# Scores of two heads at once, their low key halves as pairs of 64-row matmuls

## The chip, the cores and the metric

The kernel runs on one core of one Trainium2 chip. The metric is the device time of one execution in microseconds: from three executions the median was 1884.23 us (1883.11 to 1885.26). A separate execution was taken with the hardware profiler on; all rows below are from it.

The engines by their names in the profile: PE is the matmul engine (PEld its weight loads), DVE the vector engine, ACT the scalar engine, POOL the general one, SP issues transfers.

## The reference, cut to what matters

Two layers work on 256 tokens and 256 context tokens of width 2048: a Fourier layer and then an attention layer. The change lies in the second. Its attention has 64 query heads of width 64 in 8 groups that share one key head each. A query sees the tokens within 128 positions and all of the context, and a learned sink value joins each softmax.

```python
def _attend_with_sink(q, k, v, sink, mask=None):
    s = jnp.einsum('bqhgd,bkhd->bhgqk', q, k).astype(jnp.float32) * (ATTN_HEAD_DIM ** -0.5)
    if mask is not None:
        s = jnp.where(mask, s, NEG_INF)
    sk = jnp.broadcast_to(sink.astype(jnp.float32)[None, :, :, None, None], s.shape[:-1] + (1,))
    p = jax.nn.softmax(jnp.concatenate([s, sk], axis=-1), axis=-1)[..., :-1]
    return jnp.einsum('bhgqk,bkhd->bqhgd', p.astype(v.dtype), v)
```

The branch is multiplied by `silu(z)`, multiplied by the output weights, and added to the residual.

## The kernel before

Everything is float32. A matmul takes the reduced type `F32R`, and precision is kept by splitting an operand into a high part (`S.copy` into `F32R`, on ACT, line 60) and a low part (`V.tensor_tensor` subtract, on DVE, line 61). A product is then three matmuls (`mm3`, lines 73 to 75): high by high, high by low, low by high. Low by low is left out.

**Attention operands.** For each key head `hk`, `prep_kk` copies the 64 rows of the keys' high part into both halves of a 128-row tile `kkh`, and the low part into both halves of `kkl` (512 keys: 256 tokens, 256 context). `q_turn` makes the queries of two heads: `qa` holds the even head's high part in rows 0 to 63 and its low part in rows 64 to 127, `qb` holds the odd head's high part in rows 64 to 127 and its low part in rows 0 to 63. One 128-row matmul of `qa` by `kkh` so gives high by high plus low by high, and one of `qa` by `kkl` gives high by low plus low by low.

**Stages of one head** `i` (there are 64):

- `stage_s` (line 797): for each of two blocks of 128 queries a bank of PSUM takes the two matmuls (lines 810 and 811). DVE adds the mask and reduces the maximum (line 812, with a small row that reads the result). ACT takes the exponentials (Exp, line 815, twice, and `es`, line 816, once), DVE adds and inverts (817, 818), and ACT scales the two blocks (Copy, line 820). Result: the probabilities `p`.
- `stage_t` (line 823): eight transposes on PE (line 830) into two banks, then each is split into `ph` (ACT) and `pl` (DVE).
- `stage_o` (line 837): eight matmuls of the values by `ph` and `pl` (lines 844, 845) into one bank, copied out by ACT (`ot`, line 850) and added by DVE (851).

**Fillers.** Between the stages `filler()` calls `emit_unit`, which emits the next unit of other matmuls: an eighth of the query projection of the following key head (12 matmuls of 512 columns), half of a block of z (24 matmuls of 256 columns), or, at the end, a part of the output projection. Each unit needs a weight half split by `half_split` (`wh` on ACT, `wl` on DVE, 128 x 1024). A finished projection is copied by ACT (line 688) and rotated on POOL; a finished z block takes one `th` on ACT.

**Order.** The loop over `i` (line 870) emits: `stage_s(i)`, `stage_o(i - 2)`, a filler, `stage_t(i - 1)`, a filler. The tile framework schedules this program order against its own timeline when the kernel is built: an instruction may move forward past others that are not ready there. What results is one fixed order for each engine. PSUM has eight banks, all in one pool (`psum()`); the probabilities `p`, `ph` and `pl` have two buffers each for each name.

Of the kernel before, what the change touches and what calls it, by code (L numbers as in the profile page):

```python
# [16 lines left out]
P = 128  # L17
# [11 lines left out]
def tile_dit(ctx: ExitStack, tc: tile.TileContext, a: dict, out: bass.AP):  # L29
    nc = tc.nc  # L30
    V, S, PE, GP = nc.vector, nc.scalar, nc.tensor, nc.gpsimd
# [8 lines left out]
    def psum():  # L40
        return pp.tile([P, 512], F32, tag="ps", name="ps")
# [17 lines left out]
    def split(h, l, src):  # L59
        S.copy(h, src)  # L60
        V.tensor_tensor(l, src, h.bitcast(F32), op=ALU.subtract)  # L61
# [85 lines left out]
    with tc.tile_pool(name="st", reuse_waits="tile", bufs=1, side="right") as st:  # L147
# [55 lines left out]
        for nb in range(4):  # L203
# [11 lines left out]
            for j in range(4):  # L215
                o = psum()
# [93 lines left out]
    for g in range(G):  # L310
# [38 lines left out]
        if g == 0:  # L349
            o = psum()  # L350
# [79 lines left out]
    with tc.tile_pool(name="yp", reuse_waits="tile", bufs=32) as ypool:  # L430
# [19 lines left out]
        with tc.tile_pool(name="zp", reuse_waits="tile", bufs=2) as zp:  # L450
# [29 lines left out]
            for b in range(4, NB):  # L480
# [3 lines left out]
                o = psum()  # L484
# [32 lines left out]
        for i in range(32):  # L517
            sw, kg = i // 16, i % 16
            if kg == 0:
                o = [psum() for _ in range(8)]  # L520
# [29 lines left out]
    o = psum()  # L550
# [8 lines left out]
    o = psum()  # L559
# [27 lines left out]
    with tc.tile_pool(name="h1", reuse_waits="tile", bufs=16) as h1p:  # L587
# [3 lines left out]
        with tc.tile_pool(name="kvp", reuse_waits="tile", bufs=2) as kvp:  # L591
# [12 lines left out]
            o = [[psum() for _ in range(2)] for _ in range(4)]  # L604
# [25 lines left out]
            for hp in range(4):  # L630
                o = psum()
# [10 lines left out]
        with tc.tile_pool(name="at", reuse_waits="tile", bufs=2) as at:  # L642

            kk, qq, obs, szs = {}, {}, {}, {}
# [144 lines left out]
            def emit_y(blk):  # L789
                if blk not in szs or (blk, 1) not in obs or blk in ydone:  # L790
                    return
                ydone.add(blk)
                if blk % 2 == 0:
                    y1.append(act())
                V.scalar_tensor_tensor(y1[blk // 2][:, (blk % 2) * N : (blk % 2 + 1) * N], obs[blk, 1], 0.5, szs.pop(blk), op0=ALU.mult, op1=ALU.mult)

            def stage_s(i):
                hk, blk, hh = i // 8, i // 2, i % 2
                p2, pr = (blk % 4) // 2, blk % 2
                kkh, kkl = kk[hk]  # L800
                q2 = qq[hk, p2][hh]
                pt = at.tile([P, 2, 512], F32, tag="p", name="p")
                mx = at.tile([P, 2], F32, tag="mx", name="mx")
                sm = at.tile([P, 2], F32, tag="sm", name="sm")
                es = at.tile([P, 2], F32, tag="es", name="es")
                so = []
                for tb in range(2):
                    o = psum()
                    st = q2[:, (pr * 2 + tb) * P : (pr * 2 + tb + 1) * P]
                    PE.matmul(o, st, kkh, start=True, stop=False)  # L810
                    PE.matmul(o, st, kkl, start=False, stop=True)  # L811
                    V.tensor_tensor_reduce(o, o, mask[:, tb, :], -0.125, nsink[:, i : i + 1], ALU.add, ALU.min, mx[:, tb : tb + 1])  # L812
                    so.append(o)
                for tb in range(2):
                    S.activation(pt[:, tb, :], so[tb], AF.Exp, bias=mx[:, tb : tb + 1], scale=-1.0, accum_out=sm[:, tb : tb + 1])  # L815
                S.activation(es, mx, AF.Exp, bias=sink[:, i : i + 1])
                V.tensor_tensor(sm, sm, es, op=ALU.add)
                V.reciprocal(sm, sm)
                for tb in range(2):
                    S.activation(pt[:, tb, :], pt[:, tb, :], AF.Copy, scale=sm[:, tb : tb + 1])  # L820
                return pt

            def stage_t(pt):
                res = []
                for kp in range(2):
                    o = psum()
                    for kt in range(2):
                        for tb in range(2):
                            c = (kp * 2 + kt) * P
                            PE.transpose(o[:, (kt * 2 + tb) * P : (kt * 2 + tb + 1) * P], pt[:, tb, c : c + P], ident)  # L830
                    ph = at.tile([P, 512], F32R, tag="ph", name="ph")
                    pl = at.tile([P, 512], F32R, tag="pl", name="pl")
                    split(ph, pl, o)
                    res.append((ph, pl))
                return res

            def stage_o(i, pts):
                hk, blk, hh = i // 8, i // 2, i % 2
                oo = psum()
                for kb in range(4):  # L840
                    ph, pl = pts[kb // 2]
                    q = slice((kb % 2) * N, (kb % 2 + 1) * N)
                    st = v2[kb][hk // 4][:, (hk % 4) * P : (hk % 4 + 1) * P]
                    PE.matmul(oo[:, 0:N], st, ph[:, q], start=kb == 0, stop=False)  # L844
                    PE.matmul(oo[:, 0:N], st, pl[:, q], start=False, stop=kb == 3)  # L845
                if hh == 0:
                    obs[blk, 0] = at.tile([P, N], F32, tag="ob", name="ob", bufs=4)
                ob = obs[blk, 0]
                t = at.tile([64, N], F32, tag="ot", name="ot", bufs=1)
                S.copy(t, oo[64:128, 0:N])  # L850
                V.tensor_tensor(ob[hh * 64 : hh * 64 + 64, :], oo[0:64, 0:N], t, op=ALU.add)
                if hh == 1:
                    obs[blk, 1] = ob
                    emit_y(blk)
# [7 lines left out]
            def filler():  # L862
                j = slot[0]
                slot[0] += 1
                emit_unit()
                if defer and defer[0][0] + 2 < j:
                    defer.pop(0)[1]()

            pts, ptt = {}, {}
            for i in range(66):  # L870
                if i % 8 == 0:
                    while defer:
                        defer.pop(0)[1]()
                if i < 64:
                    pts[i] = stage_s(i)
                if i >= 2:
                    stage_o(i - 2, ptt.pop(i - 2))
                filler()
                if 1 <= i < 65:
                    ptt[i - 1] = stage_t(pts.pop(i - 1))  # L880
                filler()


        with tc.tile_pool(name="fin", reuse_waits="tile", bufs=1) as fp:
# [28 lines left out]
            o = [[psum() for _ in range(2)] for _ in range(2)]  # L913
# [12 lines left out]
            o = [psum() for _ in range(2)]  # L926
# [148 lines left out]
```

## Time and profile before

| | |
|---|---|
| median of three executions | 1884.23 us |
| the profiled execution | 1881.67 us |
| its span, first to last instruction | 1879.8 us |
| granted clock of PE, mean | 0.988 |
| the attention loop | about 1186 to 1715 us of the span |

A row of a group gives source line, engine, operation, output and input tile, shape and count, then busy time and the mean duration of one. A row of the timeline begins with its start in us and its duration. Matmuls are pipelined: one lasts longer than the distance to the start of the next, so it is that distance which tells what a matmul costs. Text in square brackets is idle time of the engine before the row and what ended it.

The costliest groups around the change, over the whole run:

```profile
L812 DVE CUSTOM_DVE_ANT_0 ps<-ps,mask,nsink 128x512 f32<-128x512 f32 x128 | 92.0, 753 | 10.9 <-PE ps L811 10.6
L815 ACT ACTIVATE p<-ps,mx 128x512 f32<-128x512 f32 x128 | 87.3, 687 | 21.3 <-DVE mx L812 20.3
L830 PE MATMUL ps<-ident,p 128*128 128x128 f32 x512 | 68.1, 273 | 0.2 <-ACT p L820 0.2
L844 PE MATMUL ps<-ph,act 128*128 128x256 f32 x256 | 66.9, 281 | 0.7 <-ACT ph L60 0.7
```

### The profile page before, as it was taken

To read this page: it belongs to the slowest core of one execution; us is meant where nothing else is said; L and a number is where in the kernel's file an instruction comes from. 1 tells how busy PE (TensorE), PEld (TensorE's weight loads), DVE (VectorE), ACT (ScalarE), POOL (GpSimd) and SP (SyncE) were. 2 spreads that over 40 slices of the span, in tenths; PEclk is the share of its full clock that TensorE was granted. 3 is DMA by queue.
4 is the path that set the end of the run, shared out by engine and by line. 5 is a ranking of instruction groups with operands and counts; after the bars stand their busy time and mean duration, and the time that the engine had idled before them with its cause. 6 is when DMAs were issued, how large, how long until landed. Compare 5 with 4: busy or idle time off the path is not lost.

```text
span 1879.8 us, 27439 instructions
## 1 busy us (share of the span) xinstructions
PE 1835.5 (98%) x10433; PEld 1583.7 (84%) x10433; DVE 1396.9 (74%) x2711; ACT 929.7 (49%) x1602; POOL 240.5 (13%) x206
## 2 busy tenths in 40 slices
PE   6899999999999999999999999999999999999997
PEld 4479999888888888888888787889989989998886
DVE  4469999787777789687984835788778787787455
ACT  3334444442222233324221524888888888887343
POOL 0034444200000000000000001112221220200001
PEclk8899999999999999999999999999999999999999
DMA  9965555656665546763575323333333333434543
GB/s 365 387 258 201 200 202 189 233 218 232 244 232 214 224 179 256 269 236 134 224 270 222 129 90 135 135 132 115 129 118 135 113 135 126 167 132 169 192 179 135
DMA packets 60533, 359.67 MB, mean 191 GB/s; under 512 B 7601, under 2 KB 7745, under 8 KB 25329
## 3 DMA queue, kind: packets, MB, share of 16 engines
q1 hardware_dynamic: 49104, 324.83, 46.7%
q0 software_dynamic: 6720, 25.34, 3.6%
q10 hardware_dynamic: 4576, 7.74, 1.3%
q8 instruction: 82, 1.34, 0.3%
q14 instruction: 51, 0.41, 0.1%
HBM read 345.30 MB, written 12.59 MB: 190 GB/s over the span
## 4 chain that ended last, share of the span: by engine, by line
PE 88%; DVE 4%; DMA 3%; issue 2%; ACT 1%; POOL 1%; ACTq 0%; POOLq 0%; DVEq 0%; SPq 0%
PE ps L73 25%; PE ps L74 25%; PE ps L75 25%; PE ps L830 3%; PE ps L845 2%; PE ps L844 2%; PE ps L811 1%; PE ps L810 1%; DMA raw<-in_awp 1%; DMA raw<-in_wu 1%; PE ps L180 1%; POOL wm L122 1%; DVE mt L239 1%; DVE wpl L61 1%; DVE wml L61 0%
## 5 line engine op out<-in xcount | busy, mean ns | idle before, releaser
L61 DVE TENSOR_TENSOR wl<-raw,wh 128x1024 fp32r<-128x1024 f32 x333 | 423.7, 1274 | 291.1 <-ACT wh L60 288.8
L60 ACT CAST wh<-raw 128x1024 fp32r<-128x1024 f32 x333 | 349.4, 1051 | 566.2 <-PE ps L74 507.0
L74 PE MATMUL ps<-act,wh 128*128 128x512 f32 x1024 | 398.3, 389 | 0.0
L73 PE MATMUL ps<-act,wh 128*128 128x512 f32 x1024 | 394.1, 389 | 0.0
L75 PE MATMUL ps<-act,wl 128*128 128x512 f32 x1024 | 391.1, 389 | 0.0
L73 PEld LDWEIGHTS ps<-act,wh 128*128 128x128 f32 x1024 | 192.2, 188 | 39.8
L75 PEld LDWEIGHTS ps<-act,wl 128*128 128x128 f32 x1024 | 192.2, 188 | 39.9
L74 PEld LDWEIGHTS ps<-act,wh 128*128 128x128 f32 x1024 | 192.2, 188 | 39.8
L417 DVE CUSTOM_DVE_ANT_0 raw<-raw,cb 128x512 f32<-128x512 f32 x256 | 172.5, 688 | 16.4 <-DMA raw<-in_adw 12.6
L73 PE MATMUL ps<-h,wh 128*128 128x256 f32 x512 | 147.1, 287 | 0.0
L74 PE MATMUL ps<-h,wh 128*128 128x256 f32 x512 | 144.8, 283 | 0.0
L75 PE MATMUL ps<-h,wl 128*128 128x256 f32 x512 | 144.7, 283 | 0.0
L417 DVE CUSTOM_DVE_ANT_0 junk<-raw,cb 128x512 f32<-128x512 f32 x192 | 131.7, 686 | 14.1 <-ACT cb L409 7.1
L74 PE MATMUL ps<-wl,h 128*128 128x512 f32 x320 | 125.5, 392 | 1.4 <-DVE wl L61 1.4
L73 PE MATMUL ps<-wh,h 128*128 128x512 f32 x320 | 124.7, 398 | 0.2 <-ACT h L600 0.2
L75 PE MATMUL ps<-wh,h 128*128 128x512 f32 x320 | 124.9, 392 | 0.0
L122 POOL TENSOR_TENSOR wm<-raw 128x1016 f32<-128x1016 f32 x32 | 87.7, 2740 | 195.8 <-DMA raw<-in_wu 195.3
L812 DVE CUSTOM_DVE_ANT_0 ps<-ps,mask,nsink 128x512 f32<-128x512 f32 x128 | 92.0, 753 | 10.9 <-PE ps L811 10.6
L73 PEld LDWEIGHTS ps<-h,wh 128*128 128x128 f32 x512 | 97.3, 190 | 1.3
L815 ACT ACTIVATE p<-ps,mx 128x512 f32<-128x512 f32 x128 | 87.3, 687 | 21.3 <-DVE mx L812 20.3
L74 PEld LDWEIGHTS ps<-h,wh 128*128 128x128 f32 x512 | 97.4, 190 | 0.0
L75 PEld LDWEIGHTS ps<-h,wl 128*128 128x128 f32 x512 | 97.3, 190 | 0.0
(302 smaller groups left out, 3785.3 us busy)
## 6 DMA issues: line engine op xcount, KB each, us to landing
raw<-in_wz SPq DMA_DIRECT2D x64, 1024.0 KB, 4.8
raw<-in_adw SPq DMA_DIRECT2D x64, 1024.0 KB, 4.8
raw<-in_awp SPq DMA_DIRECT2D x32, 1024.0 KB, 9.5
raw<-in_wo SPq DMA_DIRECT2D x32, 1024.0 KB, 5.5
raw<-in_wq SPq DMA_DIRECT2D x32, 1024.0 KB, 4.8
raw<-in_wu SPq DMA_DIRECT2D x32, 1016.0 KB, 5.4
raw<-in_wo1b SPq DMA_DIRECT2D x16, 1024.0 KB, 4.8
act<-in_xT POOLq DMA_DIRECT2D x32, 256.0 KB, 5.2
```

The source lines that it names most:

```text
L60: S.copy(h, src)
L61: V.tensor_tensor(l, src, h.bitcast(F32), op=ALU.subtract)
L73: PE.matmul(o, wh, xh, start=start, stop=False)
L74: PE.matmul(o, wh, xl, start=False, stop=False)
L75: PE.matmul(o, wl, xh, start=False, stop=stop)
L122: GP.tensor_tensor(m, v[:, :, 0, :], v[:, :, 1, :], op=ALU.subtract)
L417: V.tensor_tensor_reduce(junk if s == 0 and i < 3 else wf, wf, cb[:, s, kq * 512 : kq * 512 + 512], 1.0, 0.0, ALU.mult, ALU.add, acc[:, i, ...
L812: V.tensor_tensor_reduce(o, o, mask[:, tb, :], -0.125, nsink[:, i : i + 1], ALU.add, ALU.min, mx[:, tb : tb + 1])
L815: S.activation(pt[:, tb, :], so[tb], AF.Exp, bias=mx[:, tb : tb + 1], scale=-1.0, accum_out=sm[:, tb : tb + 1])
L830: PE.transpose(o[:, (kt * 2 + tb) * P : (kt * 2 + tb + 1) * P], pt[:, tb, c : c + P], ident)
L844: PE.matmul(oo[:, 0:N], st, ph[:, q], start=kb == 0, stop=False)
L845: PE.matmul(oo[:, 0:N], st, pl[:, q], start=False, stop=kb == 3)
```

## The change

`stage_s` is now called for an even `i` and makes the scores of two heads, in four banks. It first emits the four full matmuls by `kkh` (line 804 of the changed kernel). Then come four matmuls by `kkl` with 64 rows each (line 809): the high half of `qa` by rows 0 to 63 of `kkl`, the high half of `qb` by rows 64 to 127, alternating between the two heads and so between the two halves of the array. `tc.issue_after(full)` keeps them behind the last full matmul. Low by low is no longer computed for these products. The softmax of each head, unchanged, is moved into `softmax`. The loop keeps two fillers for each `i`; for an even `i` it now emits `stage_o(i - 2)`, `stage_t(i - 1)`, `stage_s(i)` for `i` and `i + 1`, and two fillers, and for an odd `i` `stage_o(i - 2)`, a filler, `stage_t(i - 1)`, a filler.

```diff
             def stage_s(i):
-                hk, blk, hh = i // 8, i // 2, i % 2
+                hk, blk = i // 8, i // 2
                 p2, pr = (blk % 4) // 2, blk % 2
                 kkh, kkl = kk[hk]
-                q2 = qq[hk, p2][hh]
+                so = [[psum() for _ in range(2)] for _ in range(2)]
+                for hh in range(2):
+                    for tb in range(2):
+                        full = PE.matmul(so[hh][tb], qq[hk, p2][hh][:, (pr * 2 + tb) * P : (pr * 2 + tb + 1) * P], kkh, start=True, stop=False).ins
+                for tb in range(2):
+                    for hh in range(2):
+                        r = slice(hh * 64, hh * 64 + 64)
+                        with tc.issue_after(full):
+                            PE.matmul(so[hh][tb], qq[hk, p2][hh][r, (pr * 2 + tb) * P : (pr * 2 + tb + 1) * P], kkl[r, :], start=False, stop=True)
+                return [softmax(i + hh, so[hh]) for hh in range(2)]
+
+            def softmax(i, so):
                 pt = at.tile([P, 2, 512], F32, tag="p", name="p")
...
-                so = []
-                for tb in range(2):
-                    o = psum()
-                    st = q2[:, (pr * 2 + tb) * P : (pr * 2 + tb + 1) * P]
-                    PE.matmul(o, st, kkh, start=True, stop=False)
-                    PE.matmul(o, st, kkl, start=False, stop=True)
+                for tb, o in enumerate(so):
                     V.tensor_tensor_reduce(o, o, mask[:, tb, :], -0.125, nsink[:, i : i + 1], ALU.add, ALU.min, mx[:, tb : tb + 1])
-                    so.append(o)
...
-                if i < 64:
-                    pts[i] = stage_s(i)
                 if i >= 2:
                     stage_o(i - 2, ptt.pop(i - 2))
+                if i % 2 == 0:
+                    if 1 <= i < 65:
+                        ptt[i - 1] = stage_t(pts.pop(i - 1))
+                    if i < 64:
+                        pts[i], pts[i + 1] = stage_s(i)
                 filler()
-                if 1 <= i < 65:
+                if i % 2 == 1 and i < 65:
                     ptt[i - 1] = stage_t(pts.pop(i - 1))
                 filler()
```

In the built order of the changed kernel, PE's instructions around the first pair of a key head read as follows (x: how many; T is the eight transposes of a head, O its output matmuls):

```
scores of the pair                 x5   (one by kkh, four by kkl)
O of the odd head of the pair before x8
filler                             x28
T of the even head                 x8
O of the even head                 x1
T of the odd head                  x8
scores of the next pair            x3
O of the even head                 x4
scores of the next pair            x5
O of the even head, of the odd one x7
```

## The prediction

> **What bounds the kernel now.** I read the page first, then the windows view over the attention stage, then what PE waited for there.
>
> ```profile
> span 1879.8 us, 27439 instructions
> PE 1835.5 (98%) x10433; PEld 1583.7 (84%) x10433; DVE 1396.9 (74%) x2711; ACT 929.7 (49%) x1602; POOL 240.5 (13%) x206
> ...
> 1182.00:1700.00 518.00, 517.32 (x3512) 477.27 (x3511) 412.47 (x788) 434.78 (x844) 90.88 (x76) 1.00 0.36 130
> ...
> PE ps L844 <- ACT ph L60: 0.7, 1, 0.7
> PE ps L845 <- DVE pl L61: 0.4, 1, 0.4
> PE ps L830 <- ACT p L820: 0.2, 1, 0.2
> ```
>
> The third row is the stage (columns: PE, PEld, DVE, ACT, POOL, granted clock): PE is busy for 517.3 of 518 us at full clock, so a matmul slot taken away there shortens the run. But ACT is at 84% and DVE at 80%, against 49% and 74% over the span: they follow because the order leaves them room. The last three rows are all that PE waited for from 1182 to 1760 us: 1.3 us.
>
> **What is taken away.** Four score matmuls of one head, then the next matmul (rows between have the same step):
>
> ```profile
> 1242.48 0.39 PE L810 MATMUL ps<-kkh,qa 128*128 128x512 f32 x1
> ...
> 1243.39 0.39 PE L73 MATMUL ps<-wh,h 128*128 128x512 f32 x1
> ```
>
> Starts, not durations, give the cost: 0.91 us for four, 0.2275 each. A pair of heads has eight slots now; afterwards four full ones and two rounds of two 64-row matmuls, if the two of a round run at once. That is 64 slots less in 32 pairs: 64 x 0.2275 = 14.6 us. No row shows two 64-row tiles. The nearest are the four 32-column tiles of layer 0: the rows below show one start for a round of four, so I take overlap as given, and no overlap (gain 0) as the other bound.
>
> **What is added: 32 excursions into another tiling of the array.** Layer 0 has such excursions: 128x256 matmuls, rounds of 128*32 tiles, and back. A merged row's start is the start of a round.
>
> ```profile
> 64.26 0.19 PEld L75 LDWEIGHTS ps<-dh,xl 128*128 128x128 f32 x1
> 64.38 0.28 PE L75 MATMUL ps<-dh,xl 128*128 128x256 f32 x1
> 64.59 0.16 PEld L180 LDWEIGHTS ps<-raw,c 128*32 128x32 f32 x8
> 64.59 0.64 PE L180 MATMUL ps<-raw,c 128*32 128x512 f32 x4
> 65.04 1.03 PE L180 MATMUL ps<-raw,c 128*32 128x512 f32 x7
> 65.47 1.03 PE L180 MATMUL ps<-raw,c 128*32 128x512 f32 x6
> 66.44 0.39 PE L73 MATMUL ps<-dh,xh 128*128 128x256 f32 x1
> 66.66 0.28 PE L74 MATMUL ps<-dl,xh 128*128 128x256 f32 x1
> 66.78 0.28 PE L75 MATMUL ps<-dh,xl 128*128 128x256 f32 x1
> ...
> 118.65 0.29 PE L75 MATMUL ps<-act,wpl 128*127 128x260 f32 x1
> 118.78 0.28 PE L73 MATMUL ps<-act 128*32 128x260 f32 x1
> 118.90 0.29 PE L74 MATMUL ps<-act 128*32 128x260 f32 x1
> ```
>
> A 256-column matmul takes a slot of 0.12 (66.66 to 66.78). Going in, 64.38 to 64.59 is 0.21: 0.09 too long, and the weights, otherwise loaded a slot ahead (64.26 for 64.38), are loaded only at 64.59. Coming out, the two rounds from 65.47 take 0.97 where 65.04 to 65.47 is 0.43 for one: 0.11 too long; then 66.44 to 66.66 is 0.22, another 0.10 for a 128-column load that nothing hid. Here the load on the way in has 128 columns too: another 0.10. Sum 0.40 each time, 32 x 0.40 = 12.8 us. The other bound is nothing: the last three rows go from 127 columns to one 32-column tile at the usual 0.12-0.13. I take 0.40, because those single tiles never alternate between places of the array and the half matmuls do.
>
> [...]
>
> **What is moved.** In the built order of the changed kernel all 32 groups of four half matmuls stand together, and each pair's scores are followed by two softmaxes on ACT at once. What matters is how soon the even head's transposes (T) and its first output matmul (O, now L849, before L844) come after the scores (S). Before, a typical head has 17.9 us of PE work between the end of its first score bank and its O. Now half of the pairs have some 8 us: in 15 of the 32, O stands directly behind T, in one more 0.5 us behind. Before, that happens once in 64 heads, at the start, where two heads' scores stand together too. That place shows the chain and its price:
>
> ```profile
> 1187.06 0.76 DVE L812 CUSTOM_DVE_ANT_0 ps<-ps,mask,nsink 128x512 f32<-128x512 f32 x1
> 1187.91 0.69 ACT L815 ACTIVATE p<-ps,mx 128x512 f32<-128x512 f32 x1 [0.84 <-DVE mx L812]
> 1188.59 0.68 ACT L815 ACTIVATE p<-ps,mx 128x512 f32<-128x512 f32 x1
> 1189.26 0.28 ACT L816 ACTIVATE es<-mx,sink 128x2 f32<-128x2 f32 x1
> 1189.44 1.03 ACT L60 CAST wh<-raw 128x1024 fp32r<-128x1024 f32 x1
> 1190.38 0.69 ACT L815 ACTIVATE p<-ps,mx 128x512 f32<-128x512 f32 x1
> 1191.90 1.33 ACT L820 ACTIVATE p<-p,sm 128x512 f32<-128x512 f32 x2
> 1193.13 1.05 ACT L60 CAST wh<-raw 128x1024 fp32r<-128x1024 f32 x1
> 1195.31 0.57 ACT L688 COPY act<-ps 128x512 f32<-128x512 f32 x1
> 1195.40 0.40 PE L810 MATMUL ps<-kkh,qa 128*128 128x512 f32 x1
> 1195.60 0.76 DVE L812 CUSTOM_DVE_ANT_0 ps<-ps,mask,nsink 128x512 f32<-128x512 f32 x1 [0.17 <-PE ps L811]
> 1197.36 0.39 PE L844 MATMUL ps<-ph,act 128*128 128x256 f32 x1 [0.68 <-ACT ph L60]
> ...
> 1302.88 0.38 ACT L782 ACTIVATE th<-ps 128x256 f32<-128x256 f32 x1
> 1308.39 0.37 ACT L850 COPY ot<-ps 64x256 f32<-64x256 f32 x1
> 1308.78 1.07 ACT L60 CAST ph<-ps 128x512 fp32r<-128x512 f32 x2
> ...
> 1230.36 0.28 PE L75 MATMUL ps<-h,wl 128*128 128x256 f32 x1
> 1230.48 1.03 PE L830 MATMUL ps<-ident,p 128*128 128x128 f32 x8
> 1231.47 0.28 PE L74 MATMUL ps<-h,wh 128*128 128x256 f32 x1
> ```
>
> From starts: Exp 0.67, es 0.18, weight cast wh 0.94, Copy 0.615, output copy ot 0.39, th 0.38, q copy (L688) 0.57, ph 0.54. From the end of a score bank to its first Exp: 0.20 (1195.40, the slot's end, to 1195.60) and 0.85 (1187.06 to 1187.91), 1.05. Eight transposes hold PE for 0.87 (1230.48 to 1231.47, less a slot of 0.12). ACT works through its built order (in the first kind of pair: Exp, Exp, ot, Exp, es, wh, Exp, es, Copy, Copy, wh, Copy, Copy, q copy, wh, ph), so O cannot start before 1.05 plus all that ACT does from the pair's first Exp to the first ph:
>
> - Six pairs (the first of a key head): 4 Exp 2.68, 2 es 0.36, 3 wh 2.82, 4 Copy 2.46, ot 0.39, q copy 0.57, ph 0.54 = 9.82, so 10.87. PE gets there after the second round of halves 0.23, eight O slots 0.96, 28 slots of 0.2275 6.37 and T 0.87 = 8.43. PE waits 2.4 us.
> - Seven pairs (the second of a key head): without the q copy, with th, one wh less, and in three of them one ot and one ph more: 8.69 or 9.62, so 9.7 or 10.7. PE: 0.23, 45 slots of 256 columns and a few O, 7.07 in all, T 0.87 = 8.17. PE waits 1.6 (four times) or 2.5 (three).
> - The very first pair 2.5; the two at the end, with few fillers left between, 3.0 and 4.1.
>
> 6 x 2.4 + 4 x 1.6 + 3 x 2.5 + 2.5 + 7.1 = 38 us. Used on the one such place before, the same sum gives a wait of 0.2 us, and the row shows 0.68, so it does not overstate. Used on a typical head before, it gives 13.7 us against 17.9 of PE work: no wait, as the rows show. Behind the waiting O stand the odd head's T, the next pair's S and all fillers, in PE's built order. In the other 16 pairs 11 us or more lie before T and 2.9 or more between T and O; there ACT keeps up. The bounds: 11 us (16 x the 0.68 seen) and 48 us (DVE's reduction or subtraction late by 0.6 each time, half a weight subtraction).
>
> Other edits: DVE, ACT and DMA issue the same work as before, at 80%, 84% and 36%, under PE. Four banks for scores at once instead of two: the built order takes them from tiles freed before the waiting O, so I cost it at nothing beyond that wait; if that fails, S waits for a pl, 0.7 us.
>
> **Sum.** 1881.67 (the profiled execution) - 14.6 + 12.8 + 38, less 16 x 0.21, since the way out of the tiling lies inside the stretch in which PE would wait anyway (3.4): 1914.5. The profiled execution lies 2.6 under the median 1884.23, so 1917.
>
> **Rivals.**
> - The switch is free (the 118 us rows; against it the 64 us rows, with alternating places): 1917 - 12.8 + 3.4 = 1908.
> - The halves do not run at once, so the change does not do what it says (for it: no row shows row tiles; against it: the column tiles' common start). 14.6 come back, of which 0.45 in 16 pairs fall into the wait (7.2): 1924.
> - On the other side: PE's wait is the bare cast latency, because ACT has its queue empty when T ends, and the switch is free: 16 x 0.68 = 11, 1884.2 - 14.6 + 11 = 1880.6. For it: the one row before; against it: ACT's 9 to 10 us of listed work in a stretch of 8. It is faster by over 0.2% once waits and switches together stay under 10.8 us.
>
> [...]
>
> **How the numbers follow.** Forecast 0.52, free switch 0.22, no overlap 0.13, the fast side 0.13 (0.08 faster, 0.05 within). About 0.2%, 3.8 us, is what a measurement of this kernel can tell. The first three are slower: 0.87. The likeliest is 1917, its own range 1904 to 1931 (waits of 30 to 48). For 8 in 10: down to the free switch with waits of 1.5 us in each of the 16 pairs (24), 1893, rounded to 1890, and up to no overlap with late DVE, 1935.
>
> **What will show it.** The half matmuls' rows: starts in twos, rounds 0.23 apart, or four starts 0.23 apart. Around them: 0.2 too long going in, 0.2 coming out. Among PE's waits: L849 on ACT's ph, 15 or 16 times, 1.5 to 4 us each, near 38 in all. ACT without a gap from the first Exp to that ph. The attention stage longer by some 33 us, everything before it unchanged. The forecast is wrong if L849 waits less than 15 us in total, or if PE's waits are on DVE or another line.

## The result, and the profile after

| | before | after |
|---|---|---|
| median | 1883.67 us (6 runs) | 1941.34 us (6 runs, 1937.29 to 1942.7) |
| the profiled execution | 1881.67 us | 1941.59 us |
| its span | 1879.8 us | 1939.6 us |
| granted clock of PE, mean | 0.988 | 0.982 |
| attention loop, first score matmul to last output matmul | 529.3 us | 591.6 us |

The change makes the kernel slower: the ratio is 1.0299, with a 95% interval of 1.0281 to 1.0316. The forecast was slower, 1917 us, with a range to 1935; the direction is right and the size is 24 us short.

The page of the changed kernel: span, busy time by engine, and the shares of the chain of work that ended last.

```profile
span 1939.6 us, 27522 instructions
...
PE 1853.8 (96%) x10433; PEld 1580.9 (82%) x10433; DVE 1389.0 (72%) x2711; ACT 926.9 (48%) x1602; POOL 231.0 (12%) x206
...
PE 81%; ACT 8%; DVE 4%; DMA 3%; issue 3%; POOL 1%; ACTq 0%; POOLq 0%; DVEq 0%; SPq 0%
```

PE runs as many matmuls as before, and its busy time is 18 us longer although no matmul was added. That is the first sign that waiting alone is not the whole story. ACT, which had 1% of the chain before, now has 8% of it.

What PE waited for from 1182 to 1800 us (line, releaser: us in total, times, longest):

```profile
PE ps L849 <- ACT ph L60: 33.8, 16, 2.4
PE ps L73 <- ACT act L60: 3.9, 1, 3.9
PE ps L835 <- ACT p L825: 0.9, 2, 0.7
...
```

Before, the same view added up to 1.3 us; now it is 40.2, with two rows of 0.8 that are left out. The first row is the wait that was forecast: 16 times, 38 us expected, 33.8 measured.

The same stretch by windows (start and end, length, then busy us of PE, PEld, DVE, ACT, POOL with counts, then the clock granted to PE):

```profile
1182.00:1300.00 118.00, 108.85 (x703) 95.63 (x703) 81.17 (x161) 89.37 (x176) 20.09 (x18) 0.97 0.31 108
1300.00:1400.00 100.00, 95.47 (x629) 84.62 (x628) 71.18 (x135) 76.17 (x146) 13.93 (x12) 0.97 0.33 117
1400.00:1500.00 100.00, 92.97 (x578) 80.73 (x577) 67.95 (x128) 71.89 (x138) 14.97 (x14) 0.98 0.35 125
1500.00:1600.00 100.00, 93.35 (x622) 82.96 (x622) 67.63 (x138) 74.60 (x150) 16.46 (x16) 0.95 0.27 96
1600.00:1700.00 100.00, 95.42 (x674) 85.75 (x673) 74.26 (x140) 77.62 (x149) 15.65 (x18) 1.00 0.41 147
1700.00:1800.00 100.00, 91.65 (x512) 77.37 (x512) 70.44 (x141) 69.95 (x143) 2.31 (x3) 0.97 0.38 137
```

The clock column was 1.00 throughout before. Now it averages 0.97, 0.97, 0.98, 0.95, 1.00 and 0.97. Each missing hundredth of 100 us is 1 us of full-speed work: 3.5 + 3 + 2 + 5 + 0 + 3 = 16.5 us. The forecast has no such term.

Four windows of 3.41 us, around the first two pairs of the second key head (same columns):

```profile
1270.46:1273.87 3.41, 1.13 (x10) 0.89 (x9) 1.98 (x2) 3.41 (x7) 2.08 (x2) 1.00 0.42 125
1273.87:1277.28 3.41, 3.41 (x15) 2.68 (x13) 1.65 (x4) 0.76 (x2) 3.41 (x4) 0.51 0.43 183
1284.11:1287.53 3.42, 1.95 (x17) 1.71 (x16) 1.31 (x2) 3.40 (x6) 0.00 (x0) 1.00 0.34 105
1287.53:1290.94 3.41, 2.46 (x17) 2.21 (x17) 3.09 (x5) 1.59 (x5) 0.00 (x0) 1.00 0.48 202
```

In the first window PE waits for ph and is busy for 1.13 us of 3.41; ACT is busy for all of it. In the next window the clock is halved (0.51), although PE then works without a gap. The wait of the second pair is no shorter, but it falls on two windows, which still have 1.95 and 2.46 us of work, and the clock stays at 1.00, there and behind. The clock records of this trace show ten such half-clock windows in the loop, each a record of 3.413 us at 0.5; the records at full clock between them last 6.8 to 177.5 us, 2 to 52 times that length. 10 x 3.41 x 0.5 = 17 us at most. Two rows inside the second window above show what it costs a matmul:

```profile
1275.38 0.63 PE L804 MATMUL ps<-kkh,qb 128*128 128x512 f32 x1
1275.81 0.41 PE L850 MATMUL ps<-pl,act 128*128 128x256 f32 x1
```

A slot of 512 columns takes 0.43 us here, from the first start to the second, where it takes 0.2275 at the full clock; one of 256 columns takes 0.21 instead of 0.12. Added up over the matmul starts of all ten windows that is about 15 us. By the starts of PE's matmuls, each of the ten follows a window with 2.14 to 3.38 us of idle time; of the windows at full clock with 1.83 us or less none is followed by one, and none lies between.

ACT in the first of these pairs (two rows of its timeline), and the PE row that waits for it:

```profile
1263.13 0.69 ACT L820 ACTIVATE p<-ps,mx 128x512 f32<-128x512 f32 x1 [2.48 <-DVE mx L818]
...
1272.49 1.07 ACT L60 CAST ph<-ps 128x512 fp32r<-128x512 f32 x2
```

```profile
1273.13 0.39 PE L849 MATMUL ps<-ph,act 128*128 128x256 f32 x1 [2.28 <-ACT ph L60]
```

Behind its first Exp no row of ACT up to ph has idle time in brackets: ACT works through its queue, and PE waits for the end of it.

The halves themselves, in the timeline of the changed kernel (start, duration):

```profile
1309.18 0.40 PE L804 MATMUL ps<-kkh,qb 128*128 128x512 f32 x1
1309.51 0.50 PE L809 MATMUL ps<-kkl,qa 64*128 64x512 f32 x1
1309.51 0.73 PE L809 MATMUL ps<-kkl,qb 64*128 64x512 f32 x2
1309.85 0.38 PE L809 MATMUL ps<-kkl,qa 64*128 64x512 f32 x1
1310.17 0.39 PE L73 MATMUL ps<-h,wh 128*128 128x256 f32 x1
1310.39 0.28 PE L74 MATMUL ps<-h,wh 128*128 128x256 f32 x1
```

The two halves of a round start together at the hundredth shown (the second row and the third; the third merges both rounds of `qb`). In the trace's own time stamps, which count nanoseconds, the two starts of the 64 rounds are 0 to 5 ns apart, with a median of 3. From the last full matmul to the first round are 0.33 us instead of 0.2275, to the second round 0.34, to the next full matmul 0.32, and that one's step is 0.22 where a 256-column matmul has 0.12: 0.10 too long each time, 0.40 per excursion.

**Where the time went.** The span is 59.8 us longer: 1.0 before the loop, 62.3 in it, 3.5 less behind it. In the loop, listed waits are 40.2 - 1.3 = 38.9 us more, the clock takes up to 17, and the halves with their excursions give 14.6 - 12.8 = 1.8 back. That is 54. Of the other 8 some 3.5 are waits counted short: at the place above PE's idle time is listed as 2.28 us, but its starts lie 2.44 further apart than a slot, and there are 22 such waits. The last 4.7 us, or some 7 with the clock's part at 15, are not assigned.

### The profile page after: what moved, and what is told of

Read it like the earlier page. It is cut to its first block, busy times and chain, and to the rows that moved or that the text cites. A ratio compares the mean times of both kernels' runs of the same rounds, so it can differ in the third digit from the quotient of the medians.

```text
span 1939.6 us, 27522 instructions
## 1 busy us (share of the span) xinstructions
PE 1853.8 (96%) x10433; PEld 1580.9 (82%) x10433; DVE 1389.0 (72%) x2711; ACT 926.9 (48%) x1602; POOL 231.0 (12%) x206
## 4 chain that ended last, share of the span: by engine, by line
PE 81%; ACT 8%; DVE 4%; DMA 3%; issue 3%; POOL 1%; ACTq 0%; POOLq 0%; DVEq 0%; SPq 0%
PE ps L73 24%; PE ps L74 23%; PE ps L75 23%; PE ps L835 2%; ACT p L820 2%; ACT p L825 2%; PE ps L804 2%; ACT wh L60 2%; PE ps L850 1%; PE ps L849 1%; DMA raw<-in_awp 1%; PE ps L180 1%; DMA raw<-in_wu 1%; PE ps L809 1%; POOL wm L122 1%
## 5 line engine op out<-in xcount | busy, mean ns | idle before, releaser
L61 DVE TENSOR_TENSOR wl<-raw,wh 128x1024 fp32r<-128x1024 f32 x333 | 414.8, 1247 | 338.5 <-ACT wh L60 325.9
L73 PE MATMUL ps<-act,wh 128*128 128x512 f32 x1024 | 394.0, 389 | 0.0
L73 PEld LDWEIGHTS ps<-act,wh 128*128 128x128 f32 x1024 | 192.3, 188 | 39.8
L73 PE MATMUL ps<-h,wh 128*128 128x256 f32 x512 | 146.3, 286 | 0.0
L73 PE MATMUL ps<-wh,h 128*128 128x512 f32 x320 | 122.0, 392 | 0.2 <-ACT h L600 0.2
L849 PE MATMUL ps<-ph,act 128*128 128x256 f32 x256 | 71.6, 301 | 33.8 <-ACT ph L60 33.8
L61 DVE TENSOR_TENSOR pl<-ps,ph 128x512 fp32r<-128x512 f32 x128 | 84.4, 686 | 24.3 <-ACT ph L60 24.0
L60 ACT CAST ph<-ps 128x512 fp32r<-128x512 f32 x128 | 71.3, 590 | 61.6 <-PE ps L849 48.1
L73 PEld LDWEIGHTS ps<-h,wh 128*128 128x128 f32 x512 | 97.7, 191 | 3.3 <-DVE th L783 2.6
```

What stands on the lines that cost most here:

```text
L73: PE.matmul(o, wh, xh, start=start, stop=False)
```

## The experiments

Ten kernels were run. Ratios are to the kernel before in the same session; "waits" are PE's on ph, and "loop" runs from first score matmul to last output matmul.

| run | median us | ratio (95% interval) | waits, times | lost to the clock in the loop | loop us |
|---|---|---|---|---|---|
| the changed kernel | 1941.34 | 1.0299 (1.0281 to 1.0316) | 33.8, 16 | 17.1 | 591.6 |
| full_rows | 1933.92 | 1.0259 (1.0237 to 1.0280) | 31.6, 16 | 11.9 | 586.2 |
| filled_wait | 1925.27 | 1.0224 (1.0200 to 1.0248) | 0 | 5.1 | 578.0 |
| old_loop_halves | 1904.95 | 1.0104 (1.0085 to 1.0122) | 11.9, 11 | 5.1 | 552.4 |
| old_loop_full | 1899.92 | 1.0085 (1.0066 to 1.0104) | 9.8, 10 | 5.1 | 551.1 |
| output_later | 1931.0 | 1.0245 (1.0222 to 1.0268) | 7.9, 12 | 10.2 | 578.8 |
| ph_sooner | 1954.01 | 1.0375 (1.0357 to 1.0392) | 23.9, 25 | 13.7 | 604.2 |
| two_trips | 1905.27 | 1.0115 (1.0098 to 1.0132) | 4.5, 10 | 3.4 | 553.9 |
| short_copy | 1909.07 | 1.0108 (1.0090 to 1.0126) | 15.2, 15 | 1.7 | 554.6 |
| dve_scale | 1904.6 | 1.0086 (1.0070 to 1.0102) | 8.0, 9 | 1.7 | 551.0 |
| old_loop_dve | 1903.53 | 1.0079 (1.0061 to 1.0097) | 2.5, 3 | 5.1 | 548.5 |

The loss to the clock is the length of the half-clock windows in the loop times a half; this is an upper bound, as the matmul starts give about 15 of the 17.1 in the changed kernel.

### Is it the halves? The same order with full rows

```diff
-                        r = slice(hh * 64, hh * 64 + 64)
+                        r = slice(0, 128)
```

> The changed kernel with 128 rows in the matmuls by kkl (low by low is computed again), in the same built order. Theory A (the order makes PE wait for ACT, and each long wait costs PE its clock): the waits of L849 stay near 34 us in 16 places, about ten drops of the granted clock stay, the time is 1938 to 1946 us; 64 slots come back (+14.6), the 32 excursions go (-12.8). Theory B (the two tilings in the array are what costs, by draining PE or by lowering its clock): waits or clock drops go, the time is under 1910 us.

Measured: 1933.92 us, a little under what was expected. The waits stay (31.6 us in 16), and so do the drops of the clock, seven half windows instead of ten. So almost the whole loss is there without a single half matmul: it belongs to the order. The changed kernel is 0.4% above this run, although its halves save 1.8 us; in the traces its loop is 5.4 us longer: 5.2 more of clock and 2.2 more of waiting, less what the halves save. In the changed kernel a wait that fell into one window (1.13 us of work left in it) was followed by a drop, and one no shorter that fell on two (1.95 and 2.46) was not, so no property of the halves should be read from three drops more or fewer.

### Is it PE's idle time? The wait filled with idle work

In the 16 pairs nine 128x512 matmuls, whose result is overwritten, stand behind the even head's last transpose (`last_t`). In the build the odd head's transposes and two of the next pair's scores also moved ahead of the first output matmul.

```diff
+                if hh == 0 and (blk % 4 < 2 if hk < 7 else blk % 4 >= 2):
+                    with tc.issue_after(last_t[0]):
+                        for _ in range(9):
+                            PE.matmul(oo, v2[0][hk // 4][:, 0:P], hx1[0], start=True, stop=True)
```

> The changed kernel with nine idle 128x512 matmuls (2.05 us, their result is overwritten) on PE behind the even head's transposes in the 16 pairs where PE waits. Theory A: PE's waits in the attention stage fall from 34 to under 8 us, PE works 33 us more, the granted clock stays at 1.00 through the stage, and what goes is the clock loss of some 15 us: 1920 to 1930 us. Rival (the clock drops come from the changes of tiling, or the lost clock costs nothing because ACT sets the pace): 1937 to 1945 us, clock drops unchanged.

Measured: 1925.27 us. In this kernel's waits view nothing is left on ph; all its waits are 8.9 us, 5.1 of them one wait near the end (the row shown is the largest). In its windows view the clock is whole up to 1700 us:

```profile
PE ps L837 <- ACT p L825: 7.3, 3, 5.1
```

```profile
1182.00:1700.00 518.00, 516.38 (x3472) 458.10 (x3472) 375.13 (x734) 402.48 (x789) 81.58 (x76) 1.00 0.34 121
```

144 idle matmuls of 0.2275 us are 33 us of PE work, as much as the 33.8 of waiting that they replace, and the kernel is 16 us faster than the changed one. Without the clock's part the loops are 591.6 - 17.1 = 574.5 and 578.0 - 5.1 = 572.9, equal within 2 us. But the order around the pairs moved too, so this run alone doesn't show that the 16 us come from the idle work; the next run has this order almost without it.

### Output matmul later

The same with one idle matmul instead of nine. PE's order around the pairs is that of filled_wait, so the two together separate the order from the idle work.

```diff
-                        for _ in range(9):
+                        for _ in range(1):
```

> The changed kernel with a single idle 128x512 matmul (into the output's own bank, overwritten by the output) behind the even head's transposes in the 16 pairs where the output followed them directly; in the built order the even head's first real output matmul then stands behind two or all of the odd head's transposes and two full score matmuls, some 1.2 us of work later. Theory (PE waits for ACT's ph there, and the length of the wait in one stretch decides whether the granted clock drops): each of the 16 waits shrinks from about 2.1 to about 0.9 us, 12 to 16 us in all, no drop of the granted clock falls into these pairs, and the idle matmuls cost 16 x 0.23 = 3.6 us: 1941 - 19 - 17 + 3.6 = about 1908, between 1900 and 1914. Rival (the waits are one thing, the clock's drops come from the denser score work or at random): waits shrink but the granted clock still drops about ten times, 1920 to 1928. Second rival (the loss sits in the banks and the pairing of the scores, and the wait moves to another line): 1932 or more.

Measured: 1931.0 us, far above the theory's 1908. The waits on ph did shrink, to 7.9 us, but others took their place (two of eight rows):

```profile
PE ps L855 <- ACT ph L60: 7.9, 12, 0.7
...
PE ps L804 <- ACT act L688: 4.1, 7, 0.6
```

One pair of this kernel in the timeline, PE and ACT:

```profile
1343.92 1.07 ACT L60 CAST ph<-ps 128x512 fp32r<-128x512 f32 x2
1344.56 0.38 PE L855 MATMUL ps<-ph,act 128*128 128x256 f32 x1 [0.70 <-ACT ph L60]
1344.87 0.60 ACT L688 COPY act<-ps 128x512 f32<-128x512 f32 x1
1345.52 0.50 PE L804 MATMUL ps<-kkh,qb 128*128 128x512 f32 x1 [0.58 <-ACT act L688]
```

The output waits for ph, 0.70, and the next scores wait for a bank that a query copy (L688) behind ph on ACT sets free, 0.58. So the theory was too narrow: everything behind ph in ACT's queue is late too, the wait moves on as the second rival has it (just under its 1932), and six half windows of the clock remain where none was expected. Against filled_wait the reading is plain: the same order around the pairs with 8 x 16 x 0.2275 = 29 us less PE work has a loop as long (578.8 and 578.0). In these pairs PE's work has some 30 us of room, and ACT sets the pace. It also divides the 16 us of filled_wait: the new order with one idle matmul has 10 of them already, and the eight further idle matmuls a pair bring the clock's loss from 10.2 to 5.1 us but leave the loop as long, and the two ratios (1.0245 and 1.0224) have intervals that overlap. So idle work kept the clock here; that it saves time of its own is not shown.

### Less work on ACT, PE's order kept

The four Copies of a pair that scale the probabilities cover 32 of 512 columns; most of the scaling is left out.

```diff
-                    S.activation(pt[:, tb, :], pt[:, tb, :], AF.Copy, scale=sm[:, tb : tb + 1])
+                    S.activation(pt[:, tb, 0:32], pt[:, tb, 0:32], AF.Copy, scale=sm[:, tb : tb + 1])
```

> The changed kernel with the four Copies of a pair (the softmax rows scaled by their sums) over 32 of 512 columns only, so most of the scaling is left out. The built order of PE around the 16 pairs is that of the changed kernel (eight transposes, one output matmul, eight transposes, three scores); what goes is some 4 x 0.42 = 1.7 us of ACT's work ahead of the pair's first ph (a Copy's step 0.615, the smallest ACT step in the rows about 0.2). Theory (PE waits because ACT's queue is behind by that much): the 16 waits of about 2.1 us fall to 0.4 to 0.7, 6 to 12 us in all, no wait moves to another line, and no drop of the granted clock falls into the stage before its last pairs: 1941 - 22 to 28 - 12 to 17 = 1896 to 1907. Rival (what was seen in output_later is general: the queue behind ph is as late as ph, so the waits go to the scores' banks and the outputs behind them): waits on ph small, but 1920 or more. Second rival (waits set by DVE or by latency): unchanged, 1935 or more.

Measured: ratio 1.0108; the median of 1909.07 lies 2 us above the expected range. The waits on ph are 15.2 us in 15, where 6 to 12 were expected; PE's order is kept in 15 of the 16 pairs, and some fillers elsewhere moved. ACT around the pair that starts at 1253.7 us in this kernel:

```profile
1258.23 0.96 ACT L825 ACTIVATE p<-p,sm 128x32 f32<-128x32 f32 x4
...
1261.94 0.59 ACT L688 COPY act<-ps 128x512 f32<-128x512 f32 x1 [1.21 <-PE ps L75]
1262.42 1.05 ACT L60 CAST wh<-raw 128x1024 fp32r<-128x1024 f32 x1
1263.37 0.59 ACT L688 COPY act<-ps 128x512 f32<-128x512 f32 x1
1263.85 1.09 ACT L60 CAST ph<-ps 128x512 fp32r<-128x512 f32 x2
```

Each wait is 1.0 us instead of 2.2, and that is enough for the clock: one half window remains of ten. The loop is 37 us shorter: 18.6 of listed waiting and at most 15.4 of clock are 34 of them. The wait does not fall by the whole 1.6 us that the Copies give up (their step is now 0.21, four times 0.40 less), nor to bare latency, because ACT is no longer behind from the first Exp on: it idles 1.21 us, waiting for PE's own projection, and then has a query copy, a weight cast and another query copy in its queue ahead of ph.

### The scaling on another engine

On POOL, and on DVE; all that the kernel computes stays.

```diff
-                    S.activation(pt[:, tb, :], pt[:, tb, :], AF.Copy, scale=sm[:, tb : tb + 1])
+                    GP.tensor_scalar(pt[:, tb, :], pt[:, tb, :], sm[:, tb : tb + 1], None, op0=ALU.mult)
```

> The changed kernel with the scaling of the softmax rows by their sums (two 128x512 Copies per head) moved from ACT to POOL, so that four Copies, 2.46 us, leave ACT's queue between the pair's first Exp and the first ph; the order of PE's work around these pairs also moves in the build (five output matmuls and two transposes in a row instead of one output matmul and eight transposes). Theory (the wait is ACT's work ahead of ph): the waits on ph nearly vanish, under 8 us in all, and no drop of the clock in the stage; POOL's rows of 128x512 take 1.3 us where ACT's step was 0.615, so a head's transposes come some 1.4 us later, which has cover in typical heads and may cost up to 0.7 us in the 16 pairs (11 us, as waits on POOL's p). 1941 - 26 to 34 - 17 + 0 to 11 = 1890 to 1909. Rival (the wait is not ACT's queue but the bare latency of each cast, or the scores' banks): 1930 or more, with the waits on ph still 25 us or more.

Measured: 1954.01 us, the slowest of all; the theory's numbers missed. Group and waits of this kernel:

```profile
L825 POOL TENSOR_SCALAR p<-p,sm 128x512 f32<-128x512 f32 x128 | 228.2, 1798 | 269.6 <-ACT p L820 125.7 <-ACT es L821 60.3 <-DVE sm L823 50.1
```

```profile
PE ps L849 <- ACT ph L60: 23.9, 25, 2.3
PE ps L835 <- POOL p L825: 13.4, 9, 1.7
```

One multiplication takes 1.80 us on POOL on average, not the 1.3 assumed and not ACT's step of 0.615. Four in a row take over 7 us, the transposes wait for them (13.4), and ph and pl behind the transposes are late again. This run does not decide between the theories: it replaced one late engine by a later one.

With `V.tensor_scalar` in the same place:

> The changed kernel with the scaling done by DVE instead of ACT: four 128x512 multiplications of about 0.5 us (the nearest row, a 128x512 multiplication by a column on DVE, took 0.48) go from ACT's queue, 2.46 us, to DVE's, 2.0 us a pair. The order around the 16 pairs is that of the changed kernel in the first twelve or so. Theory (ACT's queue): waits on ph fall to bare latency, 10 us in all, as in short_copy, but DVE, at 73% in the stage, now stands ahead of the transposes and of pl; 3 to 10 us of waits on DVE's p or pl appear: 1900 to 1915. Rival (DVE becomes the bound, its multiplications queued behind the weights' subtractions of 1.24 us): 1920 to 1945, with the waits on DVE lines over 20 us.

Measured: 1904.6 us, ratio 1.0086, as the theory has it, and the rival falls:

```profile
PE ps L849 <- ACT ph L60: 8.0, 9, 1.1
PE ps L850 <- DVE pl L61: 3.7, 5, 1.1
```

```profile
1182.00:1700.00 518.00, 510.24 (x3461) 454.35 (x3460) 445.99 (x883) 354.07 (x703) 81.80 (x76) 1.00 0.35 127
```

ACT goes from 389.6 busy us in this stretch in the changed kernel to 354.1 while PE does more, DVE goes to 446 of 518, and 37 us of the changed kernel's time are gone. It is the fastest of those that keep the change's own loop and all of the computation, and still slower than the kernel before.

### The old place in the loop

Scores of a pair are issued where a head's were before, ahead of the output stage, with three buffers for `p` and three instead of four for `qa` and `qb`. One kernel has the halves, the other full rows in the same built order.

```diff
+                if i % 2 == 0 and i < 64:
+                    pts[i], pts[i + 1] = stage_s(i)
                 if i >= 2:
                     stage_o(i - 2, ptt.pop(i - 2))
-                if i % 2 == 0:
-                    if 1 <= i < 65:
-                        ptt[i - 1] = stage_t(pts.pop(i - 1))
-                    if i < 64:
-                        pts[i], pts[i + 1] = stage_s(i)
                 filler()
-                if i % 2 == 1 and i < 65:
+                if 1 <= i < 65:
                     ptt[i - 1] = stage_t(pts.pop(i - 1))
...
```

> The half matmuls in pairs as changed, but the loop of before (scores first, a filler between transposes and output), with three buffers for p and three instead of four for qa and qb. Theory A: few waits of PE (under 8 us), no clock drop in the stage, starts in twos; 64 slots less (-14.6) and 32 excursions of 0.40 (+12.8): 1.8 us below old_loop_full. Theory B: the clock drops stay, 1900 us or more.

> The same with 128 rows in the matmuls by kkl, same built order. Theory A: 1.8 us (0 to 4) above old_loop_halves and within 8 us of before. If the switch were free, old_loop_halves would be 14.6 us faster than this one.

The waits with halves (with full rows 9.8 us on ph, in the table):

```profile
PE ps L849 <- ACT ph L60: 11.9, 11, 1.6
PE ps L850 <- DVE pl L61: 2.2, 2, 1.5
```

With halves 1904.95 us: moving the scores back, with these buffers, takes away 36 of the 58 us. The waits are 12 to 15 us, not under 8, but none reaches 1.8 us, and the clock is whole until the last pairs (1.00 from 1182 to 1700 us); so neither theory holds whole, since the time lies in theory B's range while of the drops that B needs only three half windows at the end are there. With full rows 1899.92, which is 16 us above the kernel before and not within 8: the halves were expected to be 1.8 us faster and are 5.0 slower, with intervals that overlap. In the traces the two loops differ by 1.3 us; the other 3.7 lie before the first score matmul, where nothing was changed. By the starts of PE's matmuls the halves do save 1.6 us of slots here; 2 us more of waiting on ph take it back, as they would if ph came no sooner when PE does. What is left against the kernel before, 0.85% with full rows, belongs to the pairing, with its buffers, and not to the halves.

With the scaling on DVE besides:

> The paired halves with scores issued at the old place in the loop (old_loop_halves) and the scaling on DVE: the remaining waits there, 12 us on ph and 2 on pl, and the three drops of the clock at the end of the stage (5 us) are what stands between it and the kernel before. Theory: the waits fall to 3 to 8 us, the drops to 0 to 2, and it comes to 1888 to 1897, ratio 1.002 to 1.008; since the halves' own gain is 14.6 - 12.8 = 1.8 us at best, it isn't faster than the kernel before by anything that can be measured. Rival (DVE's queue takes ACT's place): 1903 or more.

Measured: 1903.53 us, ratio 1.0079; the theory expected 1.002 to 1.008 and 1888 to 1897 us. The waits did not go, they changed engines:

```profile
PE ps L849 <- DVE pl L61: 7.2, 6, 1.2
PE ps L849 <- ACT ph L60: 2.5, 3, 1.1
PE ps L850 <- DVE pl L61: 2.2, 2, 1.1
```

11.9 us on ph and 2.2 on pl became 2.5 and 9.4: here the rival is right that DVE takes ACT's place. In these two kernels the pair's burst of softmax work goes through one of the two, and PE waits 14.1 and 11.9 us for it.

### What a switch costs

Two excursions per pair, each with one round of halves, instead of one with two rounds.

```diff
-                for hh in range(2):
-                    for tb in range(2):
-                        full = ...
                 for tb in range(2):
+                    for hh in range(2):
+                        full = ...
                     for hh in range(2):
```

> The halves with scores issued at the old place in the loop (as in the run old_loop_halves), but each pair's scores split by blocks of tokens: two full matmuls, one round of two halves, two full, one round of two halves. That makes two excursions into the half tiling per pair instead of one, with the same number of matmuls. By the rows of the changed kernel an excursion has 0.10 going in, 0.10 coming out and 0.10 over the step of a round for each round; the rounds stay 64, so what is added is 32 x 0.20 = 6.4 us of slots, less what lies inside waits: 3 to 7 us above old_loop_halves (ratio to the kernel before 1.012 to 1.014). Rival (an excursion costs its whole 0.40 whatever its rounds): 32 x 0.40 = 12.8 us above, 1.017. Second rival (a switch costs nothing and the slow steps belong to the half matmuls alone): no difference, 1.010, with the steps in and out at 0.23 and 0.12.

One excursion in the timeline of this kernel (L808 are the halves):

```profile
1314.52 0.39 PE L804 MATMUL ps<-kkh,qb 128*128 128x512 f32 x1
1314.84 0.49 PE L808 MATMUL ps<-kkl,qa 64*128 64x512 f32 x1
1314.84 0.49 PE L808 MATMUL ps<-kkl,qb 64*128 64x512 f32 x1
1315.26 0.50 PE L804 MATMUL ps<-kkh,qa 128*128 128x512 f32 x1
1315.60 0.40 PE L73 MATMUL ps<-wh,h 128*128 128x512 f32 x1
```

In: 0.32, 0.10 too long. The round and the way out: 0.42, 0.19 too long. The next full matmul's step: 0.34, 0.11 too long. So a trip with one round costs 0.40, as one with two rounds did above: by the rows the first rival of the expectation is right, and its 12.8 us more of slots are there. The time hardly shows them: ratio 1.0115 against 1.0104, with overlapping intervals, and a loop 1.5 us longer. In its place the waits on ph are 7.4 us shorter, those on pl 1.1 and the clock's loss 1.7: 12.8 less 10.2 is 2.6. In these two kernels most of the slots given to PE came off its waiting and its loss to the clock: 10.2 of 12.8 us. (The build also moved other instructions, so the whole alone would not price a switch; the rows do.)

## Why the forecast was right in direction and short in size

- **The waits (38 us in 16 places).** Right. L849 waits 16 times, 33.8 us; 14 of these are 2.13 to 2.42 us, where 1.6 to 2.5 was worked out. The six first pairs are close (2.28 against 2.4); the seven second ones were split into four of 1.6 and three of 2.5, and no such split is there, so in them the sum is right partly by luck. The two at the end were put at 7.1 and are 1.77 and 0.28; a wait of 3.9 us on another line (L73) came there instead. The mechanism, ACT's queue ahead of ph, is shown by short_copy, where PE's order is kept in 15 of the 16 pairs, ACT has less to do, and 18.6 us of waiting go. In the pair above ACT takes 9.90 us from its first Exp to the end of the first ph (1263.13 to 1272.49 + 0.54), where 9.82 was summed.
- **The excursions (0.40 each) and the halves (one start for a round).** The sum is right to the hundredth, its parts are not: 0.20 was put on the way in, where 0.10 is seen, and the other 0.10 lies between the two rounds, which were to start 0.23 apart and start 0.34 apart. So part of this agreement is luck; still the rivals of a free switch and of no overlap fall, and with 33.8 us of waiting the one on the other side too. That means also that the change had nothing to win: 14.6 less 12.8 is 0.1% of the run.
- **The step that failed is the sum.** "- 14.6 + 12.8 + 38, less 16 x 0.21" prices a wait at its own length and takes PE's other work at the full clock that it had before. But in the changed kernel each of the ten windows of 3.41 us at full clock in which PE idled for 2.14 us or more was followed by one at half clock, and that cost some 1.5 us more, 1.7 at most. Ten windows are 15 to 17 us, the largest part of the 27 between the growth that was forecast (1914.5 - 1881.67 = 32.8) and that of the span (59.8). The longer slots in the ten windows show it directly. short_copy shortens the wait to 1.0 us, and nine of the ten drops go; in full_rows, in the same order and with waits 2.2 us shorter, three drops fewer go with a loop that is 5.4 us shorter. filled_wait and output_later, which share one order, have three half windows with the waits filled and six without; their loops are equally long, so this pair shows what brings the drops and does not price them.
- **The rest, 10 us** (12 with the clock at 15): listed waits of 38.9 where 38 - 3.4 = 34.6 was put (4.3, for waits on other lines), the part that the listing counts short (3.5), and the 4.7 that are not assigned; 2.5 were saved outside the loop. Holds around the scores' four banks, which the forecast costed at nothing, may be in the 4.7, but no run singled them out.
- **The bounds.** The upper one, 48 us of waiting, held; the range ended at 1935 because the clock was in no bound. The likeliest range was not added up right either: by the prediction's own sum waits of 30 and 48 us give 1909 and 1927, not the 1904 and 1931 that stand there.

## What to carry to other kernels

A kernel whose PE hardly waits (1.3 us in the kernel before) can still stand at its limit on the engine behind it: before gathering two heads' scores, sum that engine's queue from the first score to the value that PE needs next, since here the burst and not the mean load of 84% decided. Price PE's waits window by window, of 3.41 us in this trace, not in sum: here 15 waits of 1.0 us came with one drop of the clock in the loop (short_copy), and one of 2.3 us inside a window cost some 1.5 us beyond its length. An excursion into half-array matmuls has 0.40 us of its own here against 0.455 saved by its two rounds, so it needs more rounds in a row than the banks for scores allowed here before it can show in the time.

## What the hardware showed that was not expected

- The clock: halved for 3.41 us after a window with 1.13 us of PE work, whole after windows with 1.95 and 2.46. In the loop of the changed kernel, among windows at the full clock, the ten with 2.14 to 3.38 us of idle time (by the starts of PE's matmuls) were each followed by a drop and none with 1.83 or less; none lies between. In the kernel before, no window from 1182 to 1760 us has more than 1.6 us of idle time, and the clock is 1.00 there.
- At half clock a slot did not double: 512 columns went from 0.2275 to 0.43 us, 256 from 0.12 to 0.21, so a whole window cost about 1.5 us and not 1.7.
- A trip to the half matmuls cost 0.40 us with one round in it and with two.
- The kernel with nine useless matmuls in each wait was 16 us faster than the changed one; 10 of these came with the order that moved, and the loop was as long with one useless matmul as with nine (578.8 and 578.0 us).
- POOL needed 1.80 us on average for a 128x512 multiplication by a column, 2.9 times ACT's step of 0.615; for DVE an estimate is 0.48, from the 61.9 us by which its busy time in dve_scale exceeds that in the changed kernel (1450.9 and 1389.0) with 128 instructions more.
